# A gated linear unit on one core: the second tile loaded row by row

## The chip, the core and the metric

The kernel runs on one core of a Trainium2 chip. Four of the core's engines matter here: ScalarE (ACT in the profile), VectorE (DVE), GpSimd (POOL) and SyncE (SP). Data moves between the chip's memory (HBM) and the core's working memory (SBUF, 128 partitions) by transfers that run on 16 DMA engines. An engine issues a transfer and goes on; a semaphore tells when the transfer has landed. The metric is the device time of one execution in microseconds (us). Three runs of the kernel before took 932.44, 932.53 and 932.56 us; the median is 932.53.

## The reference

```python
def setup_inputs():
    return {"x": np.random.randn(8192, 8192).astype(np.float32)}

def reference(x):
    a, b = np.split(x, 2, axis=-1)
    return a * (1 / (1 + np.exp(-b)))
```

Each row of 8192 numbers is cut into a left half `a` and a right half `b`, and the output row is `a` times the sigmoid of `b`. In all 268.44 MB are read and 134.22 MB written.

## The kernel before

**Tiles.** The 8192 rows are cut into 32 tiles of 256 rows. A tile gives each of the 128 partitions two rows that lie next to each other in HBM, so a whole tile is 64 KB in one piece for each partition, 8 MB in all; its output is 32 KB for each partition. There are two input slots (`x_sb0`, `x_sb1`) and two output slots (`o_sb0`, `o_sb1`); even tiles use the first of each, odd tiles the second.

**Pieces.** A tile counts as eight units, four for each of its two rows. The lists `loads`, `works` and `stores` (L33 to L39) say for each tile in which pieces it is loaded, worked on and stored: `whole` is one piece of all eight units, `rows` is one piece for each of the two rows. Tile 0 is loaded and stored by rows and worked on in fourths. The last tile is worked on in fourths and stored in three pieces. Every other tile, tile 1 among them, is loaded whole, worked on in two pieces that both span the two rows (the first 3/16 of the columns, then the rest: `few_and_most`) and stored whole.

**Work.** For each piece, `work` (L72) runs a sigmoid on ACT in place over `b` (L82) and a product into the output slot (L84). The product is done on DVE, but from tile 2 on the small first piece goes to POOL.

**Order and waits.** SP issues all loads and ACT issues all stores; these are two DMA queues, q1 and q10 in the profile. At the start the loads of tiles 0 and 1 are issued. Then for each tile `i` the program does its work, issues the load of tile `i + 2` into the slot that has come free, and the store of tile `i` (L93 to L103). A load waits for the products of the tile that was in its slot (L62). A sigmoid waits for the loads of its tile that meet its piece (L78); from tile 1 to tile 30 it also waits until the store that used the same output slot has landed (L79 to L81), in place of the product. A store waits for its products (L69).

**Start and end.** `_launch_early` moves the first load ahead of the barrier at the start of the program, and `_close_on_sync` arranges the end so that SP waits for the last store. The change touches neither.

Of the kernel before, what the change touches and what calls it, by code (L numbers as in the profile page):

```python
# [8 lines left out]
def _tiles(ctx, tc, x, out):  # L9
    nc = tc.nc  # L10
    P = nc.NUM_PARTITIONS
    DEP = mybir.DependencyInfo(mybir.DependencyClass.Sync, mybir.DependencyReason.DATA)
    fp32 = mybir.dt.float32
    SIG = mybir.ActivationFunctionType.Sigmoid

    n_rows, n_cols = x.shape
    half = n_cols // 2
    R = 2
    SLOTS = 2
    n_tiles = n_rows // (P * R)  # L20
    x_g = x.rearrange("(g p h r) m -> g h p (r m)", p=P, h=2, r=R)
    out_g = out.rearrange("(g p h r) m -> g h p (r m)", p=P, h=2, r=R)

    pool = ctx.enter_context(tc.tile_pool(name="io", bufs=1))
    xs = [pool.tile([P, R * n_cols], fp32, name=f"x_sb{k}") for k in range(SLOTS)]
    os = [pool.tile([P, R * half], fp32, name=f"o_sb{k}") for k in range(SLOTS)]

    whole = [(0, 8)]
    rows = [(0, 4), (4, 8)]
    cut = half // 16 * 3  # L30
    few_and_most = [(0, 8, 0, cut), (0, 8, cut, half)]
    fourths = [(k, k + 2, k % 4 * half // 4, (k % 4 + 2) * half // 4) for k in range(0, 8, 2)]
    loads = [whole] * n_tiles  # L33
    works = [few_and_most] * n_tiles
    stores = [whole] * n_tiles
    behind = [0] * n_tiles
    loads[0] = stores[0] = rows
    works[0] = works[-1] = fourths
    stores[-1] = [(0, 4), (4, 6), (6, 8)]  # L39
    behind[-1] = 1  # L40

    def meet(a, b):
        return a[0] < b[1] and b[0] < a[1]

    traced = [[] for _ in range(SLOTS)]
    load_of, mul_of, store_of = {}, {}, {}

    def place(i, ins, *needs):


        kept = {n.ins.name for n in needs}
        for e in traced[i % SLOTS]:
            if e.ins.name not in kept:
                tc.declare_no_dep(ins.ins, e.ins, reason="follows from the waits that are kept")
        traced[i % SLOTS].append(ins)
        tc.keep_in_program_order(ins)
        return ins

    def load(i):
        for lo, hi in loads[i]:  # L60
            c = slice(lo * n_cols // 4, hi * n_cols // 4)
            free = [m for w, m in mul_of.get(i - SLOTS, []) if meet(w, (lo, hi))]  # L62
            ins = nc.sync.dma_start(out=xs[i % SLOTS][:, c], in_=x_g[i // 2, i % 2, :, c])  # L63
            load_of.setdefault(i, []).append(((lo, hi), place(i, ins, *free)))

    def store(i, lo, hi):
        c = slice(lo * half // 4, hi * half // 4)
        ins = nc.scalar.dma_start(out=out_g[i // 2, i % 2, :, c], in_=os[i % SLOTS][:, c])  # L68
        done = [m for w, m in mul_of[i] if meet(w, (lo, hi))]  # L69
        store_of.setdefault(i, []).append(((lo, hi), place(i, ins, *done)))  # L70

    def work(i, lo, hi, near, far):  # L72

        rows = xs[i % SLOTS].rearrange("p (r h m) -> p r h m", r=R, h=2)
        packed = os[i % SLOTS].rearrange("p (r m) -> p r m", r=R)
        r, c = slice(lo // 4, (hi + 3) // 4), slice(near, far)
        b = rows[:, r, 1, c]
        landed = [s for w, s in load_of[i] if meet(w, (lo, hi))]  # L78
        gone = [s for w, s in store_of.get(i - SLOTS, []) if meet(w, (lo, hi))]  # L79
        by_sigmoid = 0 < i < n_tiles - 1  # L80
        needs = [*landed, *(gone if by_sigmoid else ())]  # L81
        sig = place(i, nc.scalar.activation(out=b, in_=b, func=SIG), *needs)  # L82
        engine = nc.gpsimd if far == cut and i > 1 else nc.vector
        mul = engine.tensor_mul(out=packed[:, r, c], in0=rows[:, r, 0, c], in1=b)  # L84
        if by_sigmoid:
            for s in gone:
                tc.add_manual_dep(sig.ins, s.ins.name, DEP, reason="frees the output slot")
        place(i, mul, sig, *(() if by_sigmoid else gone))
        mul_of.setdefault(i, []).append(((lo, hi), mul))

    for i in range(SLOTS):
        load(i)
    for i in range(n_tiles):  # L93
        due = list(stores[i])
        for k, piece in enumerate(works[i]):
            work(i, *piece)
            ready = works[i][k - behind[i]][1] if k >= behind[i] else 0
            while len(stores[i]) > 1 and k < len(works[i]) - 1 and due[0][1] <= ready:
                store(i, *due.pop(0))
        if i + SLOTS < n_tiles:  # L100
            load(i + SLOTS)
        for lo, hi in due:
            store(i, lo, hi)  # L103
# [71 lines left out]
@with_exitstack  # L175
def kernel(
    ctx: ExitStack,
    tc: tile.TileContext,
    x: bass.AP,
    out: bass.AP,  # L180
):
    nc = tc.nc
    with ExitStack() as pools:
        _tiles(pools, tc, x, out)
    tc.close()
    tc.compile()
    _launch_early(nc)
    _close_on_sync(nc)
# [30 lines left out]
```

## Time and profile before

| | |
|---|---|
| median of three runs | 932.53 us |
| the profiled execution | 932.5 us |
| its span, first to last instruction | 931.1 us |
| DVE, ACT, POOL busy | 232.5, 229.8, 99.9 us |
| loads on SP's queue | 33: two of 4 MB, 31 of 8 MB |
| stores on ACT's queue | 35: 30 of 4 MB, three of 2 MB, two of 1 MB |
| HBM over the span | 432 GB/s |

All times in the profile are counted from the span's start. A row of the timeline gives the start, the duration, the engine, the line of the kernel, the operation, the tile written and the tile read, and in brackets how long the engine had been idle and what ended that. Rows with ACTq or SPq are issues of transfers: their duration is that of the issue, not of the transfer. The DMA row of the page gives the busy share of the 16 DMA engines in 40 slices of the span, in tenths, where 9 is 90% or more. The trace also holds a record of each DMA packet with its queue, size, start and duration.

### The profile page before, as it was taken

The numbers are of one execution on the slowest core, as the hardware profiler recorded it, in microseconds if no ns is written. First come the engines' busy times: TensorE is split into PE (matmuls) and PEld (weight loads), VectorE is DVE, ScalarE is ACT, GpSimd is POOL, SyncE is SP. The second block draws the span as 40 slices with busy tenths as digits, with TensorE's granted clock in tenths as the row PEclk, the third lists the DMA queues.
The fourth block names the chain that finished last, engine by engine and source line by source line (L and its number), as shares of the span: only waits on it lengthen the run. The fifth ranks groups of instructions, "written<-read, shape, count | busy, mean of one in ns | idle before, by whom it ended". The sixth has DMA issues, their size and how long they took to land.

```text
span 931.1 us, 325 instructions
## 1 busy us (share of the span) xinstructions
DVE 232.5 (25%) x39; ACT 229.8 (25%) x69; POOL 99.9 (11%) x33
## 2 busy tenths in 40 slices
DVE  1133311333113331133320333203332033320233
ACT  2123332033320333203332023320233302333023
POOL 0001111011110111101111011110111101111010
DMA  9999999999999999999999999999999999999998
GB/s 405 450 439 417 428 450 424 455 405 428 450 428 450 407 469 409 428 450 427 452 405 450 428 428 450 424 452 408 428 450 428 450 408 465 411 428 450 427 452 383
DMA packets 9793, 402.67 MB, mean 432 GB/s; under 512 B 1088, under 2 KB 1088, under 8 KB 1088
## 3 DMA queue, kind: packets, MB, share of 16 engines
q1 hardware_dynamic: 4752, 268.44, 66.6%
q10 hardware_dynamic: 5040, 134.22, 33.4%
q14 instruction: 1, 0.01, 0.0%
HBM read 268.44 MB, written 134.22 MB: 432 GB/s over the span
## 4 chain that ended last, share of the span: by engine, by line
DMA 75%; DVE 12%; ACT 12%; issue 0%; ACTq 0%; SPq 0%
DMA out_dram<-o_sb 65%; DVE o_sb L84 12%; ACT x_sb L82 12%; DMA x_sb<-in_x_dram 10%; ACTq L68 0%; SPq L63 0%
## 5 line engine op out<-in xcount | busy, mean ns | idle before, releaser
L84 DVE TENSOR_TENSOR o_sb<-x_sb 128x6656 f32<-128x6656 f32 (+2 forms) x39 | 232.5, 5970 | 690.2 <-ACT x_sb L82 690.2
L82 ACT ACTIVATE x_sb<-x_sb 128x1536 f32<-128x1536 f32 (+1 forms) x68 | 228.5, 3407 | 689.9 <-DMA out_dram<-o_sb 630.0
L84 POOL TENSOR_TENSOR o_sb<-x_sb 128x1536 f32<-128x1536 f32 x29 | 99.7, 3437 | 787.7 <-ACT x_sb L82 787.7
L82 ACT ACT_TABLE_LOAD x1 | 1.3, 1283 | 0.8 <-PEq L203 0.8
L203 POOL MEMSET const-float32-0.0<- 128x1 f32 x1 | 0.1, 98 | 0.2 <-issue 0.2
L203 POOL MEMSET const-bfloat16-1.0<- 128x1 bf16 x1 | 0.1, 101 | 0.0
L203 POOL MEMSET const-uint8-127<- 128x1 uint8 x1 | 0.1, 101 | 0.0
L203 POOL MEMSET const-float32-1.0<- 128x1 f32 x1 | 0.1, 98 | 0.0
## 6 DMA issues: line engine op xcount, KB each, us to landing
out_dram<-o_sb ACTq DMA_DIRECT2D x30, 4096.0 KB, 43.6
x_sb<-in_x_dram SPq DMA_DIRECT2D x2, 4096.0 KB, 16.4
out_dram<-o_sb ACTq DMA_DIRECT2D x3, 2048.0 KB, 28.0
out_dram<-o_sb ACTq DMA_DIRECT2D x2, 1024.0 KB, 8.3
x_sb<-in_x_dram SPq DMA_DIRECT2D x31, 43.5
```

What stands on the lines that cost most here:

```text
L82: sig = place(i, nc.scalar.activation(out=b, in_=b, func=SIG), *needs)
L84: mul = engine.tensor_mul(out=packed[:, r, c], in0=rows[:, r, 0, c], in1=b)
L203: nc = _bacc.Bacc("TRN2", target_bir_lowering=False, num_devices=1)
```

## The change

The second tile (tile 1) is loaded in two transfers, one for each of the two rows of a partition, as the first tile is. Each of the two moves 4 MB, in pieces of 32 KB for each partition. How the tile is worked on and stored stays as it was.

```diff
     works = [few_and_most] * n_tiles
     stores = [whole] * n_tiles
     behind = [0] * n_tiles
-    loads[0] = stores[0] = rows
+    loads[0] = loads[1] = stores[0] = rows
     works[0] = works[-1] = fourths
     stores[-1] = [(0, 4), (4, 6), (6, 8)]
     behind[-1] = 1
```

In the built program SP has one more transfer at its start; the instructions of the other engines are the same. Transfers take their semaphores in turn from eight, so from the added one on each transfer uses the next semaphore: the load of tile 3 now also waits on the semaphore that the first transfer of tile 0 used, and the sigmoid of tile 1 waits on two semaphores in place of one.

## The prediction

> **What bounds the kernel now.** I read the page first, for the load of each engine and of the DMA queues.
>
> ```profile
> span 931.1 us, 325 instructions
> ...
> DVE 232.5 (25%) x39; ACT 229.8 (25%) x69; POOL 99.9 (11%) x33
> ...
> DMA  9999999999999999999999999999999999999998
> ...
> q1 hardware_dynamic: 4752, 268.44, 66.6%
> q10 hardware_dynamic: 5040, 134.22, 33.4%
> ...
> DMA 75%; DVE 12%; ACT 12%; issue 0%; ACTq 0%; SPq 0%
> ```
>
> The queue that loads (q1) and the one that stores (q10) together take 66.6 + 33.4 = 100% of the 16 DMA engines; no compute engine passes 25%. The chain in the last line gives DVE and ACT 12% each, but that is only how one tile is passed on: while one tile is worked on, the transfers of the other keep the DMA engines busy. The windows show it by stage (DMA share, GB/s in the last two columns; a packet counts where it starts, so a share can pass 1).
>
> ```profile
> 0.00:21.00 21.00, 4.49 (x2) 4.99 (x3) 0.20 (x4) 1.00 0.97 406
> 21.00:70.00 49.00, 13.35 (x4) 10.83 (x4) 0.00 (x0) 1.00 1.03 444
> 70.00:99.00 29.00, 7.09 (x1) 7.12 (x2) 3.43 (x1) 1.00 1.00 434
> 99.00:900.00 801.00, 198.58 (x28) 199.42 (x56) 96.24 (x28) 1.00 1.00 434
> 900.00:931.10 31.10, 8.99 (x4) 7.42 (x4) 0.00 (x0) 1.00 0.93 398
> ```
>
> In every stage the transfers fill the DMA engines. By the packet records of the trace each engine is idle for 0.3 to 0.6 us in all between its first packet (1.0 us) and its last (end near 930.8). So a change moves the time only if it alters the sum of the packets' durations or opens a gap on the DMA engines. Where the second tile stands is read from the timeline of the start:
>
> ```profile
> 11.98 3.71 ACT L82 ACTIVATE x_sb<-x_sb 128x2048 f32<-128x2048 f32 x2 [9.91 <-DMA x_sb<-in_x_dram]
> ...
> 18.45 0.37 ACTq L68 DMA_DIRECT2D out_dram<-o_sb  x1
> 21.68 3.71 ACT L82 ACTIVATE x_sb<-x_sb 128x2048 f32<-128x2048 f32 x2 [5.99 <-DMA x_sb<-in_x_dram]
> ...
> 28.15 0.36 ACTq L68 DMA_DIRECT2D out_dram<-o_sb  x1
> 46.29 7.12 ACT L82 ACTIVATE x_sb<-x_sb 128x1536 f32<-128x1536 f32 x2 [20.90 <-DMA x_sb<-in_x_dram]
> ...
> 60.57 0.36 ACTq L68 DMA_DIRECT2D out_dram<-o_sb  x1
> 70.71 7.12 ACT L82 ACTIVATE x_sb<-x_sb 128x1536 f32<-128x1536 f32 x2 [17.30 <-DMA out_dram<-o_sb]
> ```
>
> The two rows of tile 0 land at about 12.0 and 21.7, tile 1 at 46.3, tile 2 with the last of tile 0's stores at 70.7. The same view at the end:
>
> ```profile
> 897.20 0.34 ACTq L68 DMA_DIRECT2D out_dram<-o_sb  x1
> 911.66 5.51 ACT L82 ACTIVATE x_sb<-x_sb 128x2048 f32<-128x2048 f32 x3 [21.67 <-DMA x_sb<-in_x_dram]
> ...
> 918.13 0.34 ACTq L68 DMA_DIRECT2D out_dram<-o_sb  x1
> ```
>
> The last tile lands at 911.6 and its first store is issued at 918.13. By the packet records the store of tile 30 (issued at 897.20) runs alone from 910.7 to 920.4, and the next packet follows 0.01 us later: the tail's work is covered, with 920.42 - 918.13 = 2.29 us from issue to need.
>
> **How the queues share an engine.** The packet records show one packet of q1, then one of q10, whenever both have work, whatever their sizes. A transfer is 8 data packets on each engine (one per partition) and one small semaphore packet. From start to start a 64 KB packet takes 2.414 us, 32 KB 1.210, 16 KB 0.607.
>
> **The change, part by part.**
>
> *Packets.* Eight 64 KB packets an engine become sixteen of 32 KB: 8 x (2 x 1.210 - 2.414) = +0.05 us, and one more semaphore packet of 0.009 us. Together +0.06 us, all on the path, since the engines have no idle time to hide it. Bounds: 0, and 0.5 us if the first packet of the new transfer lasts longer as the first 64 KB packets of tile 1 do (2.48 to 2.86 us). I take 0.06; rows of one size following one another are the nearest.
>
> *SP's queue.* One more issue, 0.33 us, right behind the others at the start. What stands behind it is the load of tile 2, which waits for tile 0's last product until 28.1, so nothing is delayed. The load of tile 3 now also waits on the semaphore of tile 0's first row, long landed, and tile 1's sigmoid waits on two semaphores; a wait instruction on ACT has 17 ns. Both lie where the DMA engines are busy: nothing. If that cover were gone they would cost under 0.1 us.
>
> *Order of packets from 21.1 to 69.6.* This is what really moves. Before, loads 1 and 2 bring 16 packets of 64 KB, which alternate with tile 0's 16 store packets of 16 KB: 21.14 + 16 x (2.414 + 0.607) = 69.5 (the records have 69.65). After, load 1 alone has 16 packets, so it pairs off with all of tile 0's stores: 21.14 + 16 x (1.210 + 0.607) = 50.2. Load 2 then runs alone for 8 x 2.414 = 19.3 us, to 69.5. The same packets end at the same time; but tile 1 comes later. Before, its landing (46.27) stood 0.83 us behind the end of its round on the first engine (45.44); so now it lands at 50.2 + 0.8 = 51.0, 4.8 us later.
>
> *What is late next.* Tile 1's sigmoid (7.13 us) and product (7.10) end at about 65.3 instead of 60.55, and behind them wait load 3 on SP and store 1 on ACT. Before 69.5 they are not needed. The program's first load needs 1.0 us from issue to its first packet, and that packet 0.77 us more than the next ones: 1.8 us, so 65.3 + 1.8 = 67.1, and 2.4 us are left. Tile 2's sigmoid needs load 2 at about 70.4 (ACT free since 58.2) and starts where it did. From there the pairs (a load and a store, 29.0 us each) follow as before, each next pair queued some 14 us ahead.
>
> *Sum.* The profiled execution took 932.5 us, 1.4 more than its span of 931.1; the median of the runs shown is 932.53, so it stands for them. 932.53 + 0.06 = **932.6 us**.
>
> **The rivals.**
>
> *Stores get ahead (slower).* At 69.5 load 3 and store 1 have just been queued. If store 1 slips one or two packets of 32 KB in before load 2 has ended, that lead stays, since afterwards packets alternate strictly: each load lands 1.21 us later per packet, the last too. The stores left over then cover less: store 30 still ends at 920.4, but the first store of the last tile is issued at 919.3 or 920.6. It needs 1.0 to 1.8 us before its packets flow, so of the 2.29 us some 0.5 to 1.3 are spare. One packet costs 0 to 0.7 us, two 1.1 to 1.9: 932.6 to 933.3, or 933.7 to 934.5; with nothing spare, two cost 2.4 us (935.0). It decides from a lead of more than 0.5 us. For it: from issue at 65.3 to load 2's last packet (67.1) are 1.8 us, about what a first packet needs. Against it: tile 0's first store, issued at 18.45, was passed over by packets that began at 20.84 to 21.28, 2.4 to 2.8 us after its issue.
>
> *The DMA engines run dry at 69.5.* If tile 1 lands more than 2.4 us after 51.0, load 3 and store 1 come too late and every further microsecond is lost. Landings in the trace stand within 1 us of such a sum; 2 us late beyond the margin would give 934.6.
>
> *Each transfer costs a fixed time.* The first load landed 11.96 us after its issue, 2.3 us over its 8 x 1.210 = 9.7 us of packets; paid once more that gives 934.9. Against it: tile 0's second row, queued right behind the first, was worked on 21.68 - 11.98 = 9.70 us after it, the packets alone. The Trainium skill speaks for this rival in "DMA: Bandwidth & Descriptors", "Anatomy of one DMA": about 2.0 us fixed per DMA beside the bytes, fitted on transfers that GpSimd issues, which would make it 934.5 (an estimate by that page). The 9.70 us disagree with paying it between queued transfers.
>
> *It starts sooner (faster).* Tile 1's sigmoids span both rows and wait for both, so a first row landed early starts nothing; and all that DMA engines do not use is 931.1 less about 929.6 of packets, 1.5 us at most, which splitting does not touch. At that bound 931.0.
>
> *No effect on order:* if the engines cut 64 KB into 32 KB inside anyway, even the landing of tile 1 would stay at 46.3; 932.5.
>
> **How the numbers follow.** Forecast (with no effect on order, which gives the same) 0.55; lead of stores within one packet 0.27, of two or more 0.09; run dry 0.03; fixed cost 0.04; faster 0.02. A measurement of this kernel tells about 0.2% (1.87 us) from no change, so the bound is 934.4. Half of the two-packet case (to 934.5 and above), the dry and the fixed-cost case pass it: 0.05 + 0.03 + 0.04 = 0.12 slower, 0.02 faster, 0.86 within. The range reaches from 932.3 (the 0.3 us that an engine idles between packets gone) to 933.9, past the one-packet case and into the two-packet one; that leaves out about 0.15.
>
> **What would show it.** Right: loads on q1 x34 and 144 packets more (4896); tile 1's sigmoid at about 51 instead of 46.29 and store 1 issued at 65 instead of 60.57; tile 2's sigmoid at 70 to 71 as before; the window from 21 to 70 at the same GB/s; last tile at 911.7. The lead would show as tile 2's sigmoid 1.2 or 2.4 us late, the last tile at 912.9 or 914.1 and a dip of the DMA share near 920; running dry as a dip near 70. Wrong would be any step of DMA share below 1.0 between 21 and 900, or packets of another rate.

## The result, and the profile after

The changed kernel took 933.94 us in the median of 22 runs (932.94 to 937.39), the kernel before 932.60 us beside it (22 runs, 932.44 to 932.77). The ratio is 1.0017, with a 95% interval of 1.0011 to 1.0023: slower by 1.3 us, just under the 0.2% that the prediction had set as its bound. Two things changed. The median rose, and the times spread: the runs before lie within 0.33 us, those after over 4.5 us.

The profiled execution after took 933.35 us, in the lower part of the 22. Its page, in the lines that answer to those of before:

```profile
span 932.0 us, 328 instructions
...
DMA  9999999999999999999999999999999999999999
...
q1 hardware_dynamic: 4896, 268.44, 66.6%
q10 hardware_dynamic: 5040, 134.22, 33.4%
```

The DMA engines are still the bound, and the load queue (q1) has the 144 packets more, 4896 instead of 4752. The start of the timeline:

```profile
28.44 0.36 ACTq L68 DMA_DIRECT2D out_dram<-o_sb  x1
51.60 7.12 ACT L82 ACTIVATE x_sb<-x_sb 128x1536 f32<-128x1536 f32 x2 [25.92 <-DMA x_sb<-in_x_dram]
...
65.88 0.36 ACTq L68 DMA_DIRECT2D out_dram<-o_sb  x1
72.25 7.12 ACT L82 ACTIVATE x_sb<-x_sb 128x1536 f32<-128x1536 f32 x2 [13.53 <-DMA x_sb<-in_x_dram]
```

Tile 1 is worked on at 51.6 instead of 46.3 and its store is issued at 65.9 instead of 60.6, as forecast (51 and 65.3). But tile 2's sigmoid, forecast to start at 70 to 71 as before, starts at 72.25, 1.5 us late. At the end the lateness is still there:

```profile
899.10 0.34 ACTq L68 DMA_DIRECT2D out_dram<-o_sb  x1
913.66 5.51 ACT L82 ACTIVATE x_sb<-x_sb 128x2048 f32<-128x2048 f32 x3 [21.77 <-DMA x_sb<-in_x_dram]
...
920.12 0.34 ACTq L68 DMA_DIRECT2D out_dram<-o_sb  x1
```

The last tile's work starts 2.0 us after that of before (911.66), and its first store is issued at 920.12 instead of 918.13. What gives the cause away is one line on the DMA issues: the median time of a store from issue to landing, here before and then after.

```profile
out_dram<-o_sb ACTq DMA_DIRECT2D x30, 4096.0 KB, 43.6
```

```profile
out_dram<-o_sb ACTq DMA_DIRECT2D x30, 4096.0 KB, 39.9
```

The median store lands 3.7 us sooner after its issue, and by the packet records so does each whole store from store 2 to store 29. This is one turn of a load packet and a store packet (2.414 + 1.210 = 3.62 us), while loads take as long as before (43.6). So the stores stand one packet ahead of the loads through the whole run. The packet records show how: on every engine load 2's last data packet ends between 70.1 and 70.4 us, then one 32 KB packet of store 1 runs before load 2's semaphore packet, and a second one before load 3 begins. Before, load 3 began right behind load 2's semaphore, at 69.6 to 70.1 us. This is the first rival, the stores that get ahead.

To see where the time is lost I set, from the packet records, the moment at which the 16 engines together have moved a given number of megabytes after against the same before. The profile after is about 0.5 us behind at 16 MB and at 396 MB, and about 0.7 us at the end. So there are two places: one between 20 and 30 us, and one in the last 7 MB (after 914 us). Between them no more than 0.1 us is lost.

### The profile page after: what moved, and what is told of

It is laid out like the page before. It is cut to its first block, busy times and chain, and to the rows that moved or that the text cites. A ratio compares the mean times of both kernels' runs of the same rounds, so it can differ in the third digit from the quotient of the medians.

```text
span 932.0 us, 328 instructions
## 1 busy us (share of the span) xinstructions
DVE 232.5 (25%) x39; ACT 229.8 (25%) x69; POOL 99.9 (11%) x33
## 3 DMA queue, kind: packets, MB, share of 16 engines
q1 hardware_dynamic: 4896, 268.44, 66.6%
## 4 chain that ended last, share of the span: by engine, by line
DMA 75%; DVE 12%; ACT 12%; issue 0%; SPq 0%; ACTq 0%
DMA x_sb<-in_x_dram 75%; DVE o_sb L84 12%; ACT x_sb L82 12%; SPq L63 0%; ACTq L68 0%; ACTq L82 0%
## 6 DMA issues: line engine op xcount, KB each, us to landing
x_sb<-in_x_dram SPq DMA_DIRECT2D x30, 43.6
```

## The experiments

Theory A is the tail: the lead of the stores makes the last tile late, and a gap opens before its first store. Theory B is the start: small load packets beside small store packets. Later theories, C to H, are about the scatter; the expectation that first uses each says what it is. Each ratio is to runs of the kernel before made beside that experiment (medians 932.6 to 932.7 us), with its 95% interval.

**The changed kernel again** (no edit).

> The changed kernel once more, for a second profile and its spread. Theory A (the tail: store 1 slips one 32 KB packet ahead of the end of load 2, every later load lands 1.2 to 2 us later, and the last tile's first store is issued too late to follow store 30 without a gap) and theory B (the start: 32 KB load packets beside 16 KB store packets, from 21 to 50 us, last longer) both expect about 933.9. A expects that the profile's last tile lands 1 to 3 us after the 911.64 of before and that the time follows that landing; B expects that the excess over before is complete by 50 us.

Measured: 934.51 us in the median of 6 runs (934.08 to 937.52), before 932.65; ratio 1.0030 (1.0018 to 1.0042). The profiled execution took 934.39:

```profile
914.74 5.51 ACT L82 ACTIVATE x_sb<-x_sb 128x2048 f32<-128x2048 f32 x3 [21.82 <-DMA x_sb<-in_x_dram]
921.20 0.34 ACTq L68 DMA_DIRECT2D out_dram<-o_sb  x1
```

It is 1.04 us slower than the first profile, and its last tile is 1.08 us later. By the megabytes moved it is 0.53 us behind at 396 MB and 1.74 us at the end: the start costs about the same in both profiles, and the difference is made in the tail. The 16 engines had drifted apart in this execution (the semaphores of the last load spread over 2.1 us, against 0.83 in the first profile and 0.58 before), and a tile lands with its slowest engine. If one follows each engine's packets from end to start, it is one engine that trails: seven of its load packets, the first at 352 us, are longer by 1.5 us in sum. Windows from 920.4 to 923.4 us show the tail (busy time of DVE, ACT and POOL, the clock, then DMA share and GB/s), before, after and in this profile:

```profile
920.40:923.40 3.00, 2.29 (x1) 0.02 (x1) 0.00 (x0) 1.00 1.01 431
```

```profile
920.40:923.40 3.00, 2.84 (x2) 1.91 (x1) 0.00 (x0) 1.00 0.82 344
```

```profile
920.40:923.40 3.00, 2.97 (x2) 1.81 (x1) 0.00 (x0) 1.00 0.64 268
```

The share alone is not idle time, since a packet counts where it starts: the kernel with tile 0 in three pieces, further down, has no gap and nearly the share of the first profile after:

```profile
920.40:923.40 3.00, 2.84 (x2) 0.88 (x1) 0.00 (x0) 1.00 0.84 360
```

By the packet records between 918 and 926 us the engines are not idle at all before, each for some 0.05 us in the first profile after, and each for 1.0 us in this one. So in the first profile the lead of the stores used up the spare time and opened hardly a gap; in the second the trailing engine came on top. A holds for the part that varies. B holds for the place of a fixed half microsecond near 20 us but not for its reason: the longer load packets start between 19.7 and 21.7 us, before the first store packet runs (22.7 us).

**The tail moved ahead.**

```diff
-    stores[-1] = [(0, 4), (4, 6), (6, 8)]
+    stores[-1] = [(0, 2), (2, 4), (4, 6), (6, 8)]
```

> The changed kernel with the last tile stored in four pieces, so that its first store is issued after the first fourth, 2.26 us earlier. A: the gap near 921 is covered again; 932.9 to 933.2 (only the 0.4 us lost at the start remain), with a small spread. B: 933.9 as without the edit, since the start is untouched.

Measured: 934.26 us in the median of 11 runs (933.40 to 940.15), ratio 1.0025 (1.0014 to 1.0037). The profiled execution (933.40) did what A said: last tile at 913.63, first store issued at 917.90, and the loss of 0.76 us at 396 MB grew by less than 0.1 to the end, without a gap. But none of the 11 runs lies in A's 932.9 to 933.2: the median is hardly below the 934.51 of the changed kernel beside it, and the runs scatter up to 940. So covering the gap did not bring the times back, and something else spreads them.

**The lead taken away.** Tile 0's store is cut so that its 24 packets on each engine last until load 2 ends.

```diff
-    loads[0] = loads[1] = stores[0] = rows
+    loads[0] = loads[1] = rows
+    stores[0] = [(0, 4), (4, 6), (6, 8)]
```

> The changed kernel with tile 0 stored in three pieces, so that its store packets are 24 on each engine and pair off with the 24 load packets of tiles 1 and 2: no hole in the store queue before load 2 ends, so store 1 cannot slip ahead, although tile 1 is still loaded by rows. A: last tile lands at 911.6 to 912.2, 932.7 to 933.1. B: 933.9 or more, since small packets still run beside one another from 21 to 70.

In its profile, the stores' line of the DMA issues and the tail of the timeline:

```profile
out_dram<-o_sb ACTq DMA_DIRECT2D x30, 4096.0 KB, 43.7
```

```profile
912.52 5.51 ACT L83 ACTIVATE x_sb<-x_sb 128x2048 f32<-128x2048 f32 x3 [21.72 <-DMA x_sb<-in_x_dram]
...
918.98 0.34 ACTq L69 DMA_DIRECT2D out_dram<-o_sb  x1
```

The lead is gone (43.7 us to landing, as in the kernel before) and so is the loss in the tail: 0.65 us behind at 396 MB, 0.70 at the end. Seven of 12 runs lie at 932.99 to 933.46 (median 933.23), so with tile 1 by rows but without the lead about 0.6 us remain, a little over what A left for the start. The other five lie at 936.5 to 941.1 (median of all 933.41, ratio 1.0033, 1.0013 to 1.0053). Neither theory had foreseen these.

**A lead without the change.** Tile 1 is loaded whole; tile 0 is stored in one piece.

```diff
-    loads[0] = stores[0] = rows
+    loads[0] = rows
```

> The kernel before (tile 1 loaded whole) with tile 0 stored in one piece: its store starts later (issued at 28.1) and in 8 packets of 32 KB, so it is done near 61, and store 1 follows at once beside the last packets of load 2: a lead of about 3 packets without the change. A: last tile lands 3 to 4 us later (915 to 916), 934.5 to 936. B: 932.6, since no 32 KB load packet stands beside a 16 KB store packet after 21 us.

Measured: 935.12 us (7 runs, 934.86 to 935.60), ratio 1.0026 (1.0016 to 1.0037). These lie in A's ranges. The stores' line of the DMA issues, the tail of the timeline and the window of the gap in its profile:

```profile
out_dram<-o_sb ACTq DMA_DIRECT2D x31, 4096.0 KB, 35.0
```

```profile
915.98 5.51 ACT L82 ACTIVATE x_sb<-x_sb 128x2048 f32<-128x2048 f32 x3 [21.82 <-DMA x_sb<-in_x_dram]
...
922.45 0.34 ACTq L68 DMA_DIRECT2D out_dram<-o_sb  x1
```

```profile
920.40:923.40 3.00, 3.00 (x2) 1.66 (x2) 0.00 (x0) 1.00 0.18 76
```

The DMA engines are at 18% in these three microseconds; by the packet records each is idle for 2.3 us near 921. A kernel with tile 1 loaded whole gets the loss in the tail, larger, from the order of the queues. B's 932.6 is out, though not its place: 0.44 us were lost at the start here as well, this time behind the issue of the later store.

**Work that ends sooner.**

```diff
-    works[0] = works[-1] = fourths
+    works[0] = works[1] = works[-1] = fourths
```

(on top of the change), and the same with the last tile in four pieces.

> The changed kernel with tile 1 worked on in fourths, so that its first row is worked on when it lands (near 36 us) and the tile is done about 7 us sooner after its second row, near 58 instead of 65.9. Theory A (a hole in the store queue before load 2 ends is filled by store 1, and the lead stays to the end): store 1 enters with 3 to 5 packets of load 2 left, a lead of 3 to 5 packets; last tile lands 4 to 6 us late (915.5 to 918), gap near 921 of 2.5 to 5 us, 935.5 to 937.5: work that ends sooner makes the kernel slower. Theory B (the loss is at the start alone): 933 to 934, as the start is the same.

> The same with the last tile stored in four pieces, its first store 2.26 us sooner. A: 2.0 to 2.3 us less than without this edit, 933.5 to 935.3. B: no difference between the two.

Measured: 935.22 us (7 runs, 934.99 to 938.04), ratio 1.0032 (1.0021 to 1.0043), and 933.49 us (10 runs, 933.04 to 933.95), ratio 1.0009 (1.0000 to 1.0019). In the first one's profile, the issue of store 1 in the timeline, the stores' line of the DMA issues, and the tail of the timeline:

```profile
58.02 0.36 ACTq L68 DMA_DIRECT2D out_dram<-o_sb  x1
```

```profile
out_dram<-o_sb ACTq DMA_DIRECT2D x30, 4096.0 KB, 34.8
```

```profile
915.85 5.51 ACT L82 ACTIVATE x_sb<-x_sb 128x2048 f32<-128x2048 f32 x3 [21.83 <-DMA x_sb<-in_x_dram]
...
922.31 0.34 ACTq L68 DMA_DIRECT2D out_dram<-o_sb  x1
```

And the tail of the timeline with the last tile in four pieces:

```profile
915.92 3.71 ACT L82 ACTIVATE x_sb<-x_sb 128x2048 f32<-128x2048 f32 x2 [21.78 <-DMA x_sb<-in_x_dram]
920.19 0.34 ACTq L68 DMA_DIRECT2D out_dram<-o_sb  x1
```

Store 1 is issued 7.9 us sooner and the kernel is about a microsecond slower. The last tile lands at the same time in both, 4.2 us after that of before; storing its first fourth 2.1 us sooner brings back 1.73 us (A had 2.0 to 2.3). By the packet records each engine is idle for 2.2 us near 921 in the first and for some 0.05 us in the second. This pair shows the tail most plainly, since its runs scatter little but for one of 938.04. The stores land 8.8 us sooner after their issue than before, a lead of some 2.4 turns, below the 3 to 5 expected, and the median of the first lies just under A's range.

**The control.** The kernel before with the last tile stored in four pieces (the edit of the tail above).

> The kernel before with the last tile stored in four pieces (first store 2.26 us sooner). A: nothing to gain, since the first store already follows store 30 without a gap; 932.5 to 932.8. B has no reason for a change either; a gain of 0.3 us or more would say that the tail of the kernel before was not covered.

Measured: 932.67 us (10 runs), before 932.71; ratio 1.0000 (0.9991 to 1.0009). Without a lead the edit does nothing: the tail before was covered.

**The scatter.** Four more executions of the kernel with tile 0 in three pieces, each with its profile.

> Tile 0 stored in three pieces again, for another profile: some executions of the kernels that load tile 1 by rows took 936 to 941, and no profile of one has been seen. If one is caught: theory C (order) expects that no packet is longer than usual, that stores lead loads by 4 to 8 packets of 32 KB, that the last tile lands 5 to 9 us late and a gap of 4 to 8 us stands near 921; theory D (entry of the first store) expects the excess as longer packets between 18 and 51 us and the last tile late by the same excess, with no gap near 921. An ordinary execution is expected at 933.0 to 933.5, with 0.5 to 0.8 us lost at 18 to 24 us and no gap near 921.

> The same once more: C and D expect what they do of the look before; ordinary at 933.0 to 933.5, else 936 to 941.

> Tile 0 in three pieces once more, in search of a slow execution. E expects that a slow one (over 935) has engines whose packet order is split at 70 us (some engines' store semaphores 2 us behind the others) before any packet is long, and that an ordinary one (933.0 to 933.5) has at most a few.

> The same look again, with the same expectation as the look before: E expects split order at 70 us ahead of long packets in any execution over 935, and 933.0 to 933.5 where the order is one.

They took 953.96, 933.08, 941.67 and 933.20 us. Those near 933 are like the first profile of this kernel. Tile 2's sigmoid in the timeline of this kernel's first profile, of that of 953.96 us and of that of 941.67 us:

```profile
71.33 7.12 ACT L83 ACTIVATE x_sb<-x_sb 128x1536 f32<-128x1536 f32 x2 [14.89 <-DMA out_dram<-o_sb]
```

```profile
73.73 7.12 ACT L83 ACTIVATE x_sb<-x_sb 128x1536 f32<-128x1536 f32 x2 [17.20 <-DMA out_dram<-o_sb]
```

```profile
73.33 7.12 ACT L83 ACTIVATE x_sb<-x_sb 128x1536 f32<-128x1536 f32 x2 [17.06 <-DMA out_dram<-o_sb]
```

In the last two it waits 2.0 to 2.4 us more for tile 0's store. The packet records name the engines: in the three profiles near 933 us the semaphores of that store fall within 0.5 us on all 16 engines, in that of 953.96 us they stand at 70.4 to 70.8 on twelve engines and at 72.8 to 73.2 on four, in that of 941.67 us on 15 engines at 70.1 to 70.5 and on one at 72.8. From 35 to 75 us no packet is longer than usual in any of the five. What follows differs. In that of 953.96 us, 628 of 3824 load packets of 64 KB between 50 and 930 us were over 20 ns longer than the usual 2.418 us (one in the last profile near 933 us), 19 us for each engine in sum. In that of 941.67 us one engine trailed ever further, until the semaphores of the last load spread over 7.9 us, and the last tile came late by about that. Followed from end to start, it is the engine whose order was split at 70 us, and 51 of its load packets after 75 us are longer, by 9.0 us in sum; on the other 15 together only one is. So theory E's first half held in all five profiles of this kernel (a split order at 70 us goes ahead of both executions over 935 us, and of none of the others). Theories C and D, as they were put, are both out: packets are longer in both long executions, which C excluded, and they lie after 75 us, not before 51 as D had it. What C said of the tail did come at 941.67 us: a last tile 8 us late, and engines idle for 4 us each near 922.

A split is not enough to make an execution long. In the profile of the changed kernel with tile 1 in fourths and the last tile in four pieces (933.18 us) each store's semaphores from 120 us on stand in two groups, 13 engines and then three some 2 us later; yet only two of its load packets are longer than usual, and the ten runs of this kernel lie within 0.9 us. With tile 0 stored whole before the change the groups are 12 and four, and the seven runs lie within 0.8 us.

**Engines put out of step on purpose.** The kernel before with one more load, which writes 8 partitions of tile 1 that its own load writes again:

```diff
             load_of.setdefault(i, []).append(((lo, hi), place(i, ins, *free)))
+            if (i, lo) == (0, 0):
+                extra = nc.sync.dma_start(out=xs[1][0:8, 0:n_cols], in_=x_g[0, 1, 0:8, 0:n_cols])
+                tc.keep_in_program_order(extra)
```

> The kernel before with one more small load between tile 0's rows: 32 KB for each of partitions 0 to 7, which the whole load of tile 1 then writes again, so the result is the reference's and 0.26 MB are read twice. If it spreads over eight engines, these have one packet of 1.21 us more and stand that far behind the other eight for the whole run. Theory E (the slow executions come from engines that are out of step with one another): packets between 75 and 900 us last longer, the landings of one load spread over 2 us and more, 936 to 955 at least in some executions. Theory F (being out of step costs nothing by itself): 933.6 to 934.2, the one packet, with little spread.

Measured: 937.83 us (5 runs, 937.69 to 937.93), ratio 1.0054 (1.0042 to 1.0067). It was no clean test: around the small load the packets on all engines were longer between 11 and 17 us, 3.3 us for each engine, which neither theory had, and near 925 us the engines were idle for 1.5 us each. What it does show lies after that: the semaphores of a store then stand 1.4 to 2.0 us apart between engines through the whole run, yet from 99 to 900 us the load packets are 0.13 us longer in sum for each engine and the runs scatter by 0.24 us. Standing apart in time is not enough by itself to make packets longer.

**Store packets and load packets taken apart.** First the change with tile 0 stored whole (32 KB stores only), then the kernel before with tile 0 in three pieces (small stores, tile 1 whole).

```diff
-    loads[0] = loads[1] = stores[0] = rows
+    loads[0] = loads[1] = rows
```

```diff
-    loads[0] = stores[0] = rows
+    loads[0] = rows
+    stores[0] = [(0, 4), (4, 6), (6, 8)]
```

> The changed kernel (tile 1 by rows) with tile 0 stored in one piece: the same 32 KB load packets, now beside 8 store packets of 32 KB that start near 31 to 34 and end with load 1 near 51, so store 1 meets the end of load 2 as in the changed kernel. A (lead of one packet): the stores' median time to landing 39 to 41 us, last tile at 913 to 915, most executions 933.3 to 934.6. Theory G (the scattered executions of 936 and more come from small store packets beside 32 KB load packets, which alternate unevenly on some engines): none over 936. Theory H (they come from the 32 KB loads as such): one in six or so at 936 or more.

> The kernel before (tile 1 whole) with tile 0 stored in three pieces, 24 store packets of 16 and 8 KB beside 16 load packets of 64 KB: the store queue never runs empty before load 2 ends, so store 1 cannot get ahead. A: no lead, stores' time to landing 43 us or more, last tile at 910.5 to 912, 932.5 to 933.0. G: some executions at 936 or more, since small store packets are there. H: none, since no 32 KB load follows tile 0.

The first took 935.92 us in the median of 6 runs (934.24 to 937.88), ratio 1.0040 (1.0027 to 1.0053). Three of six are over 936, so small store packets are not needed for the scatter, and theory G falls in that form; H had expected one in six. The stores' time to landing was 43.2 us, not A's 39 to 41. That time is the slowest engine's, and here the order is split again: each store's semaphores come some 3 us later on two engines than on the other 14, which so land inside A's range. The last tile came at 914.66, inside A's 913 to 915; the median is above A's 933.3 to 934.6.

The second took 942.49 us (941.05 to 950.91), ratio 1.0118 (1.0086 to 1.0150), against 932.5 to 933.0 expected, and here the expectation had overlooked a wait. With load 1 and load 2 whole there are only 16 load packets beside 24 of tile 0's store, which so lasts beyond load 2 and slows load 3, and tile 2's sigmoid needs that store's output slot:

```profile
90.46 7.12 ACT L83 ACTIVATE x_sb<-x_sb 128x1536 f32<-128x1536 f32 x2 [36.85 <-DMA out_dram<-o_sb]
```

```profile
99.00:106.00 7.00, 5.70 (x1) 0.76 (x1) 0.00 (x0) 1.00 0.45 122
```

These are tile 2's sigmoid in the timeline and a window with the columns as above. It starts at 90 us instead of 71, load 4 and store 2 are issued at about 104.8, and the DMA engines run dry near 100 (122 GB/s in that window). That is 8.6 us by 60 MB, which makes 941.2, and three of the six runs lie there. The profiled execution took 948.09; another 6 us came in it as longer packets later. The overlooked wait spoils the test of H, but longer packets and a scatter do come here without a 32 KB load behind tile 0, so H is not the whole of it.

## Why the prediction was wrong

The forecast was 932.6 us, no change, range 932.3 to 933.9; measured were 933.94, slower by 1.3 us. The median missed the range by 0.04 us; had it just stayed inside, that would have been luck, since the order of the packets at 70 us came out another way than the forecast had it. Point by point:

- **What bounds the kernel** was right. From 21 us to the last tile the DMA engines never starve, and the profiles lose nothing between 16 and 396 MB. The window from 21 to 70 us shows 427 GB/s instead of the 444 of before, which the prediction had named as a sign of being wrong; but it counts packets where they start, and load 3's first packets, which start there on 14 engines before (69.6 to 70.0 us) and on none after, make 19 GB/s.
- **The packets** (+0.06 us) cannot be told from the rest, but 4896 packets on q1 are as forecast, and 32 KB packets last 1.213 us as those of tile 0 do.
- **The order from 21 to 70 us** was right in its times: tile 1 at 51.6 (51.0), store 1 at 65.9 (65.3), load 2's last data packet at its end at 70.1 to 70.4 (69.5).
- **"What is late next"** is the step that failed. It asked whether load 3 and store 1 come soon enough for the DMA engines not to run dry, and they do. It took the pairs after that to follow as before, though store 1, being early enough, stands at a queue with nothing ahead of it, while the load queue still has load 2's semaphore packet to deliver. Two store packets ran where the old order had none, and the first of them ahead of that semaphore. The rival that said so had 0.36 in all, with 0.27 for its one-packet case; its signs (tile 2's sigmoid 1.2 us late, the last tile at 912.9, a dip near 920) came as 1.5 us and 913.7, and the gap as 0.05 and 1.0 us of idle engines in the two profiles. Against it stood that tile 0's first store had been passed over 2.4 to 2.8 us after its issue. That did not bear on the case: store 1 was issued at 65.9 and its turn came at 70.1, 4.2 us later, when load 2's data had ended but its semaphore had not been delivered.
- **The size of that rival** was 0 to 0.7 us for one packet. The two profiles lost 0.23 and 1.2 us in the tail. The upper one is larger because one engine trailed by 1.5 us, for which no term stood.
- **The packets near 20 us** were mis-sized, and this is the other part of the miss. The prediction bounded a longer first packet of the new transfer at 0 to 0.5 us and took nothing. By the packet records the load packets that start from 18.4 to 30 us, behind the issue of the first store, are longer by 0.28 us for each engine before, and by 0.72 and 0.71 us in the two profiles of the change: 0.44 us. It is there with 64 KB loads too (0.80 us in the kernel with tile 0 stored whole, near 31 us), so the size of the load packets alone does not decide it. Already the last load packets of tile 0 (19.6 to 20.1 us), which the edit does not touch, are longer by 0.17 to 0.52 us in the mean in all ten profiles that have tile 1 by rows and a first store issued near 18.5 us, and not at all in the three that have such a store and tile 1 whole. So the way tile 1 is queued behind them bears on it; how, stays open.
- **A fixed cost for each transfer** (a chance of 0.04) did not show: the profile is about 0.5 us behind at 16 MB, which the longer packets near 20 us account for. The Trainium skill ("DMA: Bandwidth & Descriptors", "Anatomy of one DMA") has about 2.0 us for each DMA on the path that GpSimd issues; nothing near that is lost here.
- **Running dry** did not come about in the changed kernel; it did in the last experiment, where a wait moved by 20 us.

The sum that fits the profiles is 932.60 + 0.06 + 0.4 (near 20 us) + 0.2 to 1.2 (tail) = 933.3 to 934.3, around the measured median. How the median itself divides between the two is not shown, since the four pieces at the end closed the gap and left the median at 934.26. What stays open is what lengthens the packets near 20 us, and why single executions of the kernels with tile 1 by rows take 936 and more. In the two profiles of such executions, both of one variant, a split in the engines' packet order goes ahead of it, but other profiles have a split and are not long. No profile of the changed kernel itself above 935 was seen, and what splits the order was not found.

## What to carry to other kernels

When the DMA engines are full from end to end, a transfer that is moved or cut may cost little where it stands (here 0.4 us); look at which queue runs empty first afterwards, because the other queue's next packets move into the hole, and the alternation of the queues then keeps that lead to the end of the program. Its price is paid at the far end, where the last work needs a covering transfer, so count the microseconds from the issue of the last stores to the packet that they must follow. The median time from issue to landing of each queue's transfers shows such a lead in one line, and one store issued sooner can make the kernel slower.

## What the runs showed of the hardware

- Two queues alternate packet by packet on each DMA engine whatever the packets' sizes, and a semaphore packet takes a turn like a data packet: after the change one 32 KB store packet (1.21 us) ran between load 2's last data and its semaphore. The Trainium skill ("DMA: Bandwidth & Descriptors", "Queues, rings and completion order") has the alternation by packets of some 9 to 17 descriptors; here the turns change with every single record of 64, 32 or 16 KB. How many descriptors a record holds, the trace does not show.
- Load packets behind the issue of the program's first store are longer, by 0.3 to 1.0 us in sum for each engine (near 20 us, or near 31 us with tile 0 stored whole), and mostly before its first packet runs. One run is an exception: with the small extra load at the start it was 0.02 us.
- Engines that take the same packets in another order can stay apart for the whole run. Five profiled executions of one program took 933.1 to 954.0 us at a granted clock of 1.0 in all; in that of 941.67 us the load packets of a single engine, 9.0 us longer in sum, set the time.
- Around a small load to 8 partitions between two loads to 128, packets on all 16 engines were longer, by 3.3 us for each.
